# A transformer layer in fp32 on one core: the order of the first seven-fold products, the buffer of their first weight sum, and the place of eight transfers

## The chip, the core and the metric

The kernel runs on one core of one Trainium2 chip. Five engines work side by side, each through its own queue in order: PE (TensorE, matrix products), DVE (VectorE), ACT (ScalarE), POOL (GpSimd) and SP (SyncE, which here only issues transfers). POOL issues transfers too: all those that add what they carry to what lies at the target. The metric is the time of one execution in device microseconds (us); a lower one is better. Weights come from HBM (the chip's memory) in every execution.

## The reference

One layer on 512 tokens of width 2048, everything in float32, cut to what matters here:

```python
h = rms_norm(x, pre_mix_g)
z = h @ w_in                                  # [q | k | v | u], 4 x 1024 columns
a = chunked_attention(q, k, v, rel_bias)      # 8 heads
p = multiscale_pool(u, pool_w, pool_scale)    # 4 groups, windows 2, 4, 8, 16
x = x + rms_norm(concat(a, p) @ w_o, post_mix_g)
h = rms_norm(x, pre_ffn_g)
up = causal_dwconv(h @ w_up, conv_w, conv_b)  # w_up: 2048 x 11264
y = (gelu(up[..., :5632]) * up[..., 5632:]) @ w_down
x = x + rms_norm(y, post_ffn_g)
```

## The kernel before

**Numbers as pairs.** A float32 operand is split into a rounded high part and the rest: ACT writes the high part (L135, `activation` Copy), DVE subtracts it (L136). A product is then three matmuls (high by high, high by low, low by high), or two in the products of w_up. Every weight tile of 128x1024 numbers (512 KB) so costs one transfer into a raw buffer, one ACT instruction and one DVE instruction before PE can read it. Raw tiles of the tag `raw` (`raw4`, five buffers) and split halves of the tag `w4` (`w4`, eight buffers, so four pairs) are shared by all stages up to the products of w_up. A second set of raw buffers is `raw_x` (tag `x`, four buffers); the sums of h use it first, then the weights.

**Fewer products.** w_o, w_up and w_down are multiplied by the scheme of Strassen and Winograd: seven products of half-size blocks instead of eight, named by `i` = 1 to 7. Products 4, 5, 6 and 7 need sums of weight blocks. They are made in two ways:

- For w_o and for the first group of w_down, in HBM ahead of time by `sums_in_dram` (L296 on). It is a generator; each step is one transfer of 1 MB: a `copy`, issued by SP and tied behind the last weight load that SP issued (`issue_after(load_w.last)`), or an `add`, issued by POOL with `accum_op`. There are 32 steps for w_o (tile `wt`) and then 16 for w_down (tile `t`, `first_sum`): copies of sum 5 (2 steps, one for each half `cc` of the columns), adds to 5, copies of 7, copies of 6 from 5, adds to 7, adds to 6, copies of 4 from 6, adds to 4. The sums of w_down are read some 1000 us later. `more_sums(n)` takes n steps; the head loop takes the first 24.
- For w_up in SBUF by the class `Factors`. `k` numbers the 41 weight tiles that go through the scheme, `i` the product. For one `k`, the tile `x` is loaded by SP (L1089) and then added to by POOL (L1106), each time after the product's split has read the last state: product 1 reads the block as it is, 5 after one add, 6 after a second, 4 after a third. Products 3 and 7 share the tile `y` (one add between), product 2 reads `z`. Tiles `y` and `z` lie in `raw4`, `x` in `raw_x`. Only for the first and the last k (`alone`) is product 1 loaded by itself as `w`, since the order asks for 1 before the sum is there, and `x` starts with two blocks, the load and one add.

**Stages.** Projections of q, k and v with attention, head by head (to some 316 us); the eight projections of u with the pooling (`pool_proj`, `pool_keep`, `pool_mix`, to 409 us), whose running sums are chains of DVE additions with small POOL memsets between them (L488, L495); w_o (`wo_product`, seven products of two halves each, 409 to 562 us); the first three weight tiles of w_up without the scheme (`up`, to 644 us); then the loop over `factors.order`, "the sevens" (to some 1440 us); then w_down.

**The order around the change.** PE keeps the program's order; on the other engines a scheduler at build time orders instructions by when it expects them to be ready, the program's order deciding between them. In the sevens, `seven(k, i)` calls `factors.get`, which first emits the splits (`make`) up to four products ahead, then the matmuls; `keep(k, i)` after it empties the PSUM bank: after product 5 ACT copies bank `g` to `zb` (L1165), after product 6 bank `a` to `zm` (L1169). Product 3 adds onto bank `g` after product 5, product 7 onto bank `a` after 6, so each waits for that copy. The first six products are written out by hand in `begin`:

```python
begin = [(0, 1), (0, 2), (1, 1), (1, 2), (0, 5), (0, 3)]
```

and then come (0, 6), (0, 7), (1, 5), (0, 4), (1, 3), (2, 1), and so on. During the last plain product `up(1, 0)` the loads of the first six are issued and the splits of the first four made.

Of the kernel before, what the change touches and what calls it, by code (L numbers as in the profile page):

```python
# [75 lines left out]
def encoder_layer(ctx: ExitStack, tc: tile.TileContext, x, xT, vecs, rel, post_mix, post_ffn,  # L76
# [24 lines left out]
    def bank(name):  # L101
        return psum.tile([P, 512], F32, tag="ps", name=name)
# [4 lines left out]
    def raw4(name):  # L107
        return big.tile([P, 1024], F32, tag="raw", bufs=5, name=name)
# [41 lines left out]
    def mm3(ps, l, r, first, last, onto=False):  # L150
        nc.tensor.matmul(ps, l[0], r[0], start=first, stop=False, skip_group_check=onto)  # L151
        low = ps if len(r[1].shape) == 2 else ps.rearrange("p (a b) -> p a b", a=2)
        nc.tensor.matmul(low, l[0], r[1], start=False, stop=False, skip_group_check=onto)  # L153
        nc.tensor.matmul(ps, l[1], r[0], start=False, stop=last, skip_group_check=onto)  # L154
# [42 lines left out]
    def part(w, *idx):  # L197
        return tuple(v[(slice(None),) + idx] for v in w)
# [136 lines left out]
    for kb in range(KD):  # L335
        i, o = divmod(kb, 8)
        nc.sync.dma_start(xt[kb // 4][:, kb % 4, :], xT[kb * P:(kb + 1) * P, :])
        for what in "qk":
            if kb in chunks:
                raw, hi, lo = first[f"{what}0_{i}"]  # L340
# [18 lines left out]
    with tc.tile_pool(name="p1", bufs=2, reuse_waits="tile") as p1:  # L359
# [39 lines left out]
        def project(name, between=None):  # L399
            ps = bank(name)  # L400
            for i in range(2):
                if i and between:
                    between()
                w = weights.get(f"{name}_{i}")
                for j in range(8):
                    kb = 8 * i + j
                    mm3(ps, part(w, j), blk(hT, kb), kb == 0, kb == KD - 1)
            return ps
# [65 lines left out]
        def values(h):  # L474
            ps = bank(f"a{h}")
            d = slice((h % 4) * DH, (h % 4 + 1) * DH)
            for k in range(NT):
                sl = slice(PT_AT[k], PT_AT[k] + S - PT_Q[k])
                mm3(ps[:, PT_Q[k]:], part(state["v"], k, d), (pth[:, sl], ptl[:, sl]), k == 0, k == NT - 1)
            nc.scalar.activation(mix(h), ps, AF.Copy)  # L480

        def pool_proj(g, j):
            pool_keep(g, j, project(f"u{2 * g + j}"))
# [24 lines left out]
        def pool_mix(g, keep_):  # L508
            w = weights.get(f"pm{g}")
            d = [state.pop(("pool", g, a)) for a in range(2)]  # L510
            for j in range(2):
                ps = bank(f"pm{g}_{j}")
                for a in range(2):
                    mm3(ps, part(w, a, slice(j * P, (j + 1) * P)), d[a], a == 0, a == 1)
                keep_(HEADS + 2 * g + j, ps, col(V_PSCALE, 2 * g + j))
# [35 lines left out]
        def more_sums(n):  # L551
            for _ in range(n):
                next(sums_step, None)

        more_sums(2)
        pool_proj(0, 0)
        turn(6)
        scores(7)
        pool_proj(0, 1)
        more_sums(2)  # L560
        values(6)
        more_sums(2)
        pool_proj(1, 0)
        more_sums(2)
        turn(7)
        pool_proj(1, 1)
        more_sums(3)
        values(7)
        mixT += [acc8(f"mixT{i}", "B").rearrange("p (a b) -> p a b", a=4) for i in (2, 3)]
        pool_mix(0, keep_mix)  # L570
        more_sums(3)
        pool_proj(2, 0)
        more_sums(3)
        pool_proj(2, 1)
        pool_mix(1, keep_mix)
        more_sums(3)
        pool_proj(3, 0)
        more_sums(3)
        u7 = project("u7")


# [16 lines left out]
        def wo_product(i, cc, left, between=None):  # L598
            ps = [bank(f"m{i}{cc}{t}") for t in range(2)]
            if cc:  # L600
                more_sums(1)
            for q in range(4):
                w = weights.get(f"wo{i}_{cc}_{q}")
                for j in range(2):
                    kb = 2 * q + j
                    for t in range(2):
                        mm3(ps[t], tuple(v[:, kb, t * P:(t + 1) * P] for v in left), part(w, j), kb == 0, kb == 7)
                if between:
                    between(q)
            return ps  # L610
# [226 lines left out]
    def right(c, cc):  # L837
# [10 lines left out]
        while True:  # L848
            i = order
            if (c, (cc, i)) in ready_first:  # L850
                hi, lo = right_tile("wh", "bh"), right_tile("wl", "bl")
                for v, source in zip((hi, lo), ready_w[cc, i]):
                    with tc.issue_after(first_right.part) if first_right.part else nullcontext():
                        first_right.part = nc.gpsimd.dma_start(v, source.bitcast(F32R)).ins
                order = yield hi, lo
                continue
            if c == 0:

                v = first_right(cc, i, raw1 if (ORDER0.index((cc, i)) - len(ready_first)) % 5 < 3 else later["raw2"])
            else:  # L860
                for jl in {1: (11, 12), 6: (22,), 2: (21,)}.get(i, ()):
                    b[jl] = load(jl // 10 - 1, jl % 10 - 1)
                if i == 5:
                    nc.vector.tensor_add(b[11], b[11], b[12])
                if i == 7:
                    nc.vector.tensor_add(b[12], b[22], b[12])
                if i == 6:
                    nc.vector.tensor_add(b[11], b[11], b[22])
                if i == 4:
                    nc.vector.tensor_add(b[21], b[21], b[11])  # L870
                v = b[{1: 11, 5: 11, 7: 12, 6: 11, 2: 21, 3: 22, 4: 21}[i]]
            hi, lo = right_tile("wh", "bh"), right_tile("wl", "bl")
            split(hi, lo, v)
            order = yield hi, lo
# [71 lines left out]
    with tc.tile_pool(name="p3", bufs=2, reuse_waits="tile") as p3:  # L946
# [86 lines left out]
        def raw_x(name):  # L1033
            return p3.tile([P, 1024], F32, tag="x", bufs=4, name=name)
# [31 lines left out]
        class Factors:  # L1066
# [3 lines left out]
            def __init__(self):  # L1070
                n = 2 * NU - PLAIN

                self.alone = 0, n - 1
                place_of = {1: 0, 6: 8, 2: 2, 7: 10, 5: 4, 4: 12, 3: 6}
                begin = [(0, 1), (0, 2), (1, 1), (1, 2), (0, 5), (0, 3)]
                end = [(n - 1, 5), (n - 2, 6), (n - 1, 3), (n - 1, 1), (n - 2, 7), (n - 1, 6), (n - 2, 4),
                       (n - 1, 7), (n - 1, 2), (n - 1, 4)]
                order = sorted((7 * k + at, k, i) for k in range(n) for i, at in place_of.items())  # L1080
                self.order = begin + [(k, i) for _, k, i in order if (k, i) not in begin + end] + end
                self.raw, self.made, self.loaded, self.used = {}, [], 0, 0
# [4 lines left out]
            def load(self, k, i):  # L1087
                def raw(what, tile_, m, kh):
                    nc.sync.dma_start(tile_, self.block(k, m, kh))  # L1089
                    self.raw[k, what] = tile_  # L1090

                if i == 1 and (k, "w") not in self.raw:
                    raw("w" if k in self.alone else "x", raw4("wx") if k == self.alone[0] else raw_x("wx"), 0, 0)
                elif i == 5 and k == self.alone[0]:
                    raw("x", raw_x("wx"), 0, 0)
                    self.add(k, "x", 1, 0)
                elif i == 5 and k == self.alone[1]:
                    raw("w", raw_x("wx"), 0, 0)
                    raw("x", raw_x("wx"), 1, 0)
                elif i == 3:  # L1100
                    raw("y", raw4("wy"), 1, 1)
                elif i == 2:
                    raw("z", raw4("wz"), 0, 1)
# [137 lines left out]
    with tc.tile_pool(name="p4", bufs=2, reuse_waits="tile") as p4:  # L1241
# [19 lines left out]
        def left(c):  # L1261

            def load(i):
                g = half_g(f"gc{i}")
                nc.sync.dma_start(g, gd[c][i])
                return [g[:, :, j, :] for j in range(2)]

            i = yield
            a11, a12 = load(0)
            v = {1: a11, 2: a12}  # L1270
            while True:
                if 7 not in v and (c or i not in (1, 2)):
                    a21, a22 = load(1)
                    s = scratch("s")
                    v.update({5: s, 7: a21, 6: s, 3: s, 4: a22})
                if i == 5:
                    nc.vector.tensor_sub(s, a22, a21)
                if i == 6:
                    nc.vector.scalar_tensor_tensor(s, s, -1.0, a11, op0=ALU.mult, op1=ALU.subtract)
                if i == 3:  # L1280
                    nc.vector.scalar_tensor_tensor(s, a12, -1.0, s, op0=ALU.mult, op1=ALU.subtract)
                if i == 7:
                    nc.vector.tensor_sub(a21, a11, a21)
                hi, lo = slot_h("ah", F32R), slot_l("al", F32R)
                split(hi, lo, v[i])
                i = yield hi, lo
# [198 lines left out]
```

## Time and profile before

| | us |
|---|---|
| time, median of 3 runs | 1888.29 (1887.30 to 1889.62) |
| the profiled execution | 1887.21, span 1885.4 |
| PE busy / DVE busy / ACT busy / POOL busy | 1862.0 / 1438.4 / 1019.2 / 297.3 |
| PE idle from 380 to 560 us | 5.7 |
| PE idle from 645 to 690 us | 6.7 |
| PE idle from 690 to 1435 us | 0.0 |

How to read the rows below: a row of the timeline has its start and its duration in us, then engine, line, operation, output `<-` inputs and the number of instructions; in brackets the engine's idle time before it and what ended that. SPq is SP's queue, that is the issue of a transfer. The chain of waits has start, duration and what. A row of the waits has who waited for whom, the total in us, how many times, and the longest. A row of the windows has the stretch, its length, busy time and number of instructions of each engine, the granted clock of PE, the busy share of the 16 DMA engines and GB/s. A row of the transfers of a queue has packets, MB and the share of the 16 DMA engines in that stretch (q0: POOL's, q1: SP's); one of the issues has KB and the median us from issue to landing.

### The profile page before, as it was taken

How to read it: one execution, taken by the hardware profiler on the slowest of the kernel's cores; microseconds unless marked ns; L12 is line 12 of the kernel's file. 1: busy time of each engine (PE TensorE's matmuls, PEld its weight loads, DVE VectorE, ACT ScalarE, POOL GpSimd, SP SyncE). 2: the span in 40 equal slices, each digit the busy share in tenths (PEclk: the TensorE clock that was granted, in tenths of full speed). 3: DMA queues.
4: the chain of work that ended last, by engine and by line, in shares of the span. 5: the costliest groups of instructions: out<-in, count | busy, mean ns of one | idle time of the engine just before them, and what ended most of it. 6: DMA issues, size and time to landing. Idle time of an engine off the chain costs nothing.

```text
span 1885.4 us, 24890 instructions
## 1 busy us (share of the span) xinstructions
PE 1862.0 (99%) x9486; PEld 1591.7 (84%) x9486; DVE 1438.4 (76%) x1631; ACT 1019.2 (54%) x1287; POOL 297.3 (16%) x400
## 2 busy tenths in 40 slices
PE   9999999989999989999999999999999999999998
PEld 7888888868889878888888888888888888888886
DVE  5554446468598978888888888888887899889875
ACT  6433333246456456666656656665665765565553
POOL 4301011100000112222121221212211011111101
PEclk9999999999999999999999999999999999999999
DMA  8899599997665688989889888898988977877785
GB/s 293 250 252 238 155 274 273 255 246 248 222 222 202 166 185 197 200 199 209 208 196 204 200 205 202 200 211 199 204 187 275 351 233 179 204 201 174 176 236 151
DMA packets 181751, 409.20 MB, mean 217 GB/s; under 512 B 11456, under 2 KB 62528, under 8 KB 176320
## 3 DMA queue, kind: packets, MB, share of 16 engines
q0 software_dynamic: 52112, 156.78, 43.5%
q1 hardware_dynamic: 129520, 250.84, 39.8%
q8 instruction: 74, 1.21, 0.3%
q14 instruction: 45, 0.37, 0.1%
HBM read 361.44 MB, written 96.47 MB: 243 GB/s over the span
## 4 chain that ended last, share of the span: by engine, by line
PE 92%; DMA 3%; DVE 2%; issue 1%; ACT 1%; SPq 0%; POOL 0%; POOLq 0%; DVEq 0%; ACTq 0%
PE qa L159 16%; PE qa L165 8%; PE qg L159 8%; PE qg L165 4%; PE pa L151 4%; PE pa L154 4%; PE pa L153 4%; PE qd L159 4%; PE m L153 2%; PE m L154 2%; PE m L151 2%; PE qd L165 2%; PE pg L151 2%; PE pg L154 2%; PE pg L153 2%; PE v L153 2%
## 5 line engine op out<-in xcount | busy, mean ns | idle before, releaser
L135 ACT ACTIVATE wfh<-wx 128x1024 fp32r<-128x1024 f32 x164 | 173.7, 1059 | 137.6 <-PE qg L159 52.5
L159 PE MATMUL qa<-gT,wfh 128*128 128x512 f32 x984 | 246.4, 392 | 0.0
L136 DVE TENSOR_TENSOR wfl<-wx,wfh 128x1024 fp32r<-128x1024 f32 x164 | 200.5, 1222 | 57.7 <-ACT wfh L135 43.6
L159 PEld LDWEIGHTS qa<-gT,wfh 128*128 128x128 f32 x984 | 177.0, 189 | 31.7
L1106 POOL DMA_DIRECT2D wx<-in_w_up x122 | 104.6, 860 | 509.4 <-DVE wfl L136 447.0
L159 PE MATMUL qg<-h,wfh 128*128 128x512 f32 x656 | 163.6, 392 | 6.0 <-ACT zb L1165 6.0
L159 PEld LDWEIGHTS qg<-h,wfh 128*128 128x128 f32 x656 | 124.0, 189 | 32.0 <-ACT zb L1165 6.2
L136 DVE TENSOR_TENSOR bl<-b,bh 128x2048 fp32r<-128x2048 f32 x56 | 127.1, 2286 | 18.6 <-ACT bh L135 11.7
L165 PE MATMUL qa<-gT,wfl 128*128 128x256 f32 x984 | 137.8, 283 | 0.7 <-ACT zm L1169 0.7
L135 ACT ACTIVATE wfh<-wy 128x1024 fp32r<-128x1024 f32 x82 | 86.9, 1060 | 91.9 <-PE qg L159 54.6
L135 ACT ACTIVATE bh<-b 128x2048 fp32r<-128x2048 f32 x56 | 106.0, 1912 | 54.7 <-DVE b L870 22.5
L165 PEld LDWEIGHTS qa<-gT,wfl 128*128 128x128 f32 x984 | 129.4, 191 | 4.6 <-ACT zm L1169 1.3
L151 PE MATMUL pa<-bh,ah 128*128 128x512 f32 x320 | 124.5, 389 | 0.0
L153 PE MATMUL pa<-bl,ah 128*128 128x512 f32 x320 | 124.5, 389 | 0.0
L154 PE MATMUL pa<-bh,al 128*128 128x512 f32 x320 | 124.5, 389 | 0.0
L136 DVE TENSOR_TENSOR wfl<-wy,wfh 128x1024 fp32r<-128x1024 f32 x82 | 100.1, 1220 | 8.6 <-PE qa L159 2.9
L165 PEld LDWEIGHTS qg<-h,wfl 128*128 128x128 f32 x656 | 89.5, 190 | 6.5
L136 DVE TENSOR_TENSOR wfl<-wz,wfh 128x1024 fp32r<-128x1024 f32 x41 | 50.3, 1226 | 55.6 <-PE qa L159 55.6
L165 PE MATMUL qg<-h,wfl 128*128 128x256 f32 x656 | 91.5, 282 | 0.0
L159 PE MATMUL qa<-h,wfh 128*128 128x512 f32 x328 | 82.1, 392 | 0.0
L159 PE MATMUL qd<-gT,wfh 128*128 128x512 f32 x328 | 81.1, 389 | 0.0
L938 POOL DMA_DIRECT2D sum<-part x30 | 36.2, 1207 | 262.6 <-DVE part L924 190.3
(543 smaller groups left out, 4554.1 us busy)
## 6 DMA issues: line engine op xcount, KB each, us to landing
wx<-in_w_up POOLq DMA_DIRECT2D x122, 512.0 KB, 6.1
b<-in_w_down SPq DMA_DIRECT2D x32, 1024.0 KB, 7.0
wx<-in_w_up SPq DMA_DIRECT2D x43, 512.0 KB, 5.4
wz<-in_w_up SPq DMA_DIRECT2D x41, 512.0 KB, 5.9
wy<-in_w_up SPq DMA_DIRECT2D x41, 512.0 KB, 4.6
wy<-in_w_up POOLq DMA_DIRECT2D x41, 512.0 KB, 6.8
sum<-part POOLq DMA_DIRECT2D x38, 512.0 KB, 7.8
wt<-in_w_o POOLq DMA_DIRECT2D x16, 1024.0 KB, 12.7
```

Source lines behind the costliest of these rows:

```text
L135: rounded = nc.scalar.activation(hi, src, AF.Copy)
L136: rest = nc.vector.tensor_sub(lo, src, f32(hi))
L151: nc.tensor.matmul(ps, l[0], r[0], start=first, stop=False, skip_group_check=onto)
L153: nc.tensor.matmul(low, l[0], r[1], start=False, stop=False, skip_group_check=onto)
L154: nc.tensor.matmul(ps, l[1], r[0], start=False, stop=last, skip_group_check=onto)
L159: nc.tensor.matmul(ps, w[0][:, kb], pairs[kb][0], start=fresh and not kb, stop=last, skip_group_check=not fresh)
L165: nc.tensor.matmul(ps[:, sl], w[1][:, kb], pair[:, sl], start=False, stop=last, skip_group_check=not fresh)
L938: nc.gpsimd.dma_start(dest, v, accum_op=ALU.add)
L1106: nc.gpsimd.dma_start(self.raw[k, what], self.block(k, m, kh), accum_op=ALU.add)
```

## The change

Two things are edited. In the stages of u and w_o, `more_sums` is called with smaller numbers between the projections (16 steps there instead of 23), and the last eight steps are taken in the second halves of the w_o products, one in each, two in that of product 3 (before, one step was left for them). In the sevens, `begin` is reordered: (0, 5) comes third instead of fifth, and (1, 1) stands between (0, 5) and (0, 3); the tile `x` of k = 0 is taken from `raw4` instead of `raw_x`.

```diff
-        more_sums(2)
+        more_sums(1)
         pool_proj(0, 0)
...
         pool_proj(0, 1)
         more_sums(2)
         values(6)
-        more_sums(2)
+        more_sums(1)
         pool_proj(1, 0)
         more_sums(2)
         turn(7)
         pool_proj(1, 1)
-        more_sums(3)
+        more_sums(2)
         values(7)
...
         pool_mix(0, keep_mix)
-        more_sums(3)
+        more_sums(2)
         pool_proj(2, 0)
-        more_sums(3)
+        more_sums(2)
         pool_proj(2, 1)
         pool_mix(1, keep_mix)
-        more_sums(3)
+        more_sums(2)
         pool_proj(3, 0)
-        more_sums(3)
+        more_sums(2)
         u7 = project("u7")
...
             if cc:
-                more_sums(1)
+                more_sums(2 if i == 3 else 1)
...
-                begin = [(0, 1), (0, 2), (1, 1), (1, 2), (0, 5), (0, 3)]
+                begin = [(0, 1), (0, 2), (0, 5), (1, 1), (0, 3), (1, 2)]
...
                 elif i == 5 and k == self.alone[0]:
-                    raw("x", raw_x("wx"), 0, 0)
+                    raw("x", raw4("wx"), 0, 0)
                     self.add(k, "x", 1, 0)
```

## The prediction

> **What bounds the kernel now.** First the page's busy times, then who PE waited for over the whole run, then windows around those waits.
>
> ```profile
> PE 1862.0 (99%) x9486; PEld 1591.7 (84%) x9486; DVE 1438.4 (76%) x1631; ACT 1019.2 (54%) x1287; POOL 297.3 (16%) x400
> ...
> PE qg L159 <- ACT zb L1165: 6.0, 1, 6.0
> PE u L151 <- ACT u_1h L135: 1.5, 1, 1.5
> PE m L153 <- DVE wo_2l L136: 1.4, 1, 1.4
> PE u L154 <- DVE u_1l L136: 1.3, 2, 0.8
> PE m L151 <- ACT wo_2h L135: 1.1, 1, 1.1
> PE qa L165 <- ACT zm L1169: 0.7, 1, 0.7
> PE m L153 <- DVE wo_1l L136: 0.5, 1, 0.5
> ...
> 386.00:422.00 36.00, 30.26 (x122) 0.95 0.95 264
> 657.00:672.00 15.00, 8.27 (x41) 0.77 0.84 179
> ...
> 690.00:1435.00 745.00, 745.00 (x4282) 657.90 (x4281) 619.54 (x728) 453.38 (x553) 162.49 (x196) 1.00 0.88 200
> ```
>
> PE is busy 1862.0 of 1885.4 us, and from 690 to 1435 us without a gap. So only time at which PE stands still, or runs with a lower granted clock, can be won. Apart from the start and the tail, that lies in two places, and each edit touches one: 386 to 422 us (u's last projections, w_o's first product; clock 0.95) and 657 to 672 us (the start of the sevens; clock 0.77).
>
> **What the first place costs.** Five of the waits lie there: 1.5 + 1.3 + 0.5 + 1.1 + 1.4 = 5.7 us (1.3 are two waits, so six gaps). A matmul of 512 columns is written 0.39 long but the next starts 0.23 after it, so each gap of the profile hides another 0.16, and the first matmul after it takes about 0.1 more: 6 x 0.26 = 1.6 us. After the last one the clock is down:
>
> ```profile
> 420.00 0.43 PE m L153
> ...
> 422.29 0.23 PE m L154
> ```
>
> From 418.9 to 421.1 the steps are 0.43 instead of 0.23, some seven of them with the partial ones: 1.5 us. Together 8.8 us.
>
> **What it comes from.** SP's queue and POOL's queue, in order, around 343 to 402:
>
> ```profile
> SPq L300 <- DMA t<-in_w_down: 15.7, 3, 8.9
> ...
> 358.93 27.79 DMA u_1r<-in_w_in
> ...
> 387.93 0.50 PE L151 MATMUL u<-hT,u_1h 128*128 128x512 f32 x1 [1.46 <-ACT u_1h L135]
> ...
> q1 hardware_dynamic: 425, 0.21, 12.2%
> ...
> 397.99 1.16 POOL L303 DMA_DIRECT2D t<-in_w_down  x1 [19.23 <-DMA t<-t]
> ...
> 400.20 1.16 POOL L303 DMA_DIRECT2D t<-in_w_down  x1 [0.94 <-DMA t<-t]
> 401.94 0.11 POOL L488 MEMSET u<- 128x16 f32 x1 [0.48 <-DVE tmp L500]
> 399.29 0.70 DVE L493 TENSOR_TENSOR us<-us 128x524 f32<-128x524 f32 x1 [5.93 <-POOL us L495]
> ```
>
> The copies of sum 6 from 5 stand in SP's queue until the adds to 5 have landed (15.7 us in all), and the load `u_1r` of the seventh u projection, queued behind them, goes out at 358.93 and lands 27.79 later, at 386.7; PE needs it at 386.5 (387.93 less the wait). It is slow since two adds are in flight: from 376 to 384 us (the row q1) SP's queue gets 12.2% of the DMA engines and moves 0.21 MB, at which pace 512 KB take 20 us. Then the memset of a pooling chain stands behind an add that waits 19.23 us for its copy, and DVE, in order, idles 5.93 us for it. From 399.3 DVE is late; w_o's splits, and behind them PE, wait for that.
>
> **Part 1, the transfers.** After the edit the copies stand elsewhere in SP's queue: those of 5 behind the u load behind which those of 7 stand now, those of 7 behind the last u load, those of 6 behind the first load of w_o, those of 4 in w_o's products 6 and 3. Adds are tied to nothing but their copies: the one at 400.20 belongs, by the program, to w_o's product 1 and still stands ahead of a memset of the pooling before it. So I expect the adds to go as copies land, and only the two copies and two adds of sum 4 truly move into w_o. What matters is that nothing stands ahead of `u_1r` any more. Its buffer is free from
>
> ```profile
> 347.39 1.22 DVE L136 TENSOR_TENSOR u_1l<-u_1r,u_1h 128x1024 fp32r<-128x1024 f32 x1 [1.34 <-ACT u_1h L135]
> ```
>
> on, so it goes out at 348.6. If it again takes 27.8 it is there at 376.4, ten before PE asks. DVE then does not idle the 7.9 us for its split (380.0 to 387.9) nor most of the 5.93, and is some ten ahead where it was late. I take 7.9 of the 8.8 and leave 0.9 for a split that still comes late among DVE's work in w_o's first product. Bounds: 8.8, if nothing is left; 4.4, if the waits for wo_1 and wo_2 stay (3.0, their hidden part 0.8, and a part of the clock's); 0, if the crowd on the DMA engines is as before: counted by the program's steps, nine of ten copies and of ten adds stay between u's second projection and w_o's first product.
>
> The cover of the moved ones: w_o's loads.
>
> ```profile
> 503.00:545.00 42.00, 42.00 (x187) 34.75 (x187) 31.33 (x27) 20.59 (x26) 0.00 (x0) 1.00 0.56 181
> ...
> 506.31 0.38 SPq L146 DMA_DIRECT2D wo_0r<-in_w_o  x1
> 517.53 1.06 ACT L135 ACTIVATE wo_0h<-wo_0r 128x1024 fp32r<-128x1024 f32 x1 [1.66 <-PE m L153]
> 525.72 0.39 PE L151 MATMUL m<-wo_0h,s 128*128 128x512 f32 x1
> ...
> q0 software_dynamic: 594, 1.18, 83.5%
> q1 hardware_dynamic: 295, 0.58, 23.9%
> ...
> wo_1r<-in_w_o SPq DMA_DIRECT2D x1, 512.0 KB, 12.3
> ```
>
> A load goes out 19.4 us before its matmul, its two splits take 2.3, so it may take 17.1 to land. The last three rows are from 402 to 410, w_o loads under two adds: at most 12.3 us. An add of 1 MB takes 1 / 1.18 x 8 = 6.8 us, in which SP moves one load instead of the 2.5 that PE uses (one in 2.7 us): 4.1 us late, a copy the like, and the DMA engines are 44% idle to catch up. Price 0; without that cover, 4 us for each. POOL's only other work there, the two norms, is wanted after the last add, and the copies that move wait for adds issued some 100 us before, so SP's queue does not stand.
>
> **Part 2, the sevens.**
>
> ```profile
> 649.39 2.00 PE L159 MATMUL qa<-gT,wfh 128*128 128x512 f32 x8
> 652.18 2.00 PE L159 MATMUL qd<-gT,wfh 128*128 128x512 f32 x8
> ...
> 663.97 3.55 PE L159 MATMUL qg<-h,wfh 128*128 128x512 f32 x8 [6.04 <-ACT zb L1165]
> ...
> 638.81 1.04 ACT L135 ACTIVATE wfh<-wx 128x1024 fp32r<-128x1024 f32 x1
> ...
> 657.45 1.06 ACT L135 ACTIVATE wfh<-wx 128x1024 fp32r<-128x1024 f32 x1 [4.47 <-DMA wx<-in_w_up]
> 660.02 1.06 ACT L135 ACTIVATE wfh<-wy 128x1024 fp32r<-128x1024 f32 x1 [1.52 <-DMA wy<-in_w_up]
> ...
> 663.34 0.57 ACT L1165 ACTIVATE zb<-qg 128x512 f32<-128x512 f32 x1
> ...
> 608.13 6.00 SPq L1089 DMA_DIRECT2D wz<-in_w_up  x2
> 636.78 9.19 SPq L1089 DMA_DIRECT2D wx<-in_w_up  x3
> 641.86 1.86 POOL L1106 DMA_DIRECT2D wx<-in_w_up  x2 [36.30 <-DMA wx<-in_w_up]
> DMA to landing us min/median/max: 5.5/7.8/9.4
> ```
>
> A product takes 2.79 us (652.18 - 649.39). The copy `zb` of (0, 5) stands on ACT behind the splits of (0, 6) and (0, 7), which wait for adds (657.45, 660.02), and PE, at 657.8 done with (0, 5), waits until 663.97: 6.04, 0.16 hidden, and 8 matmuls at the lower clock, 3.55 instead of about 2.0: 7.8 us.
>
> After: the tile of (0, 5) takes the raw buffer that frees third, at 613.8 (second of the `wz` issues at 608.13), not 636.8, and POOL, idle 36.30 us there, adds its second block by some 625. Its split comes in third place (638.81, DVE's half done by 642.2); its next add is issued at 642.3 and lands 5.5 to 9.4 later (last row, that tile from 640 to 660 us): 647.8 to 651.7. (0, 5) runs 649.4 to 652.2, PE having begun the sevens at 643.8 (two products earlier), and the last split ahead of `zb` on ACT is that of (0, 6): done by 652.8, `zb` by 653.4. PE has (1, 1) in between and asks for it at 655.0: no wait, 1.6 us to spare. The same products in the same number: nothing is added.
>
> What is late next: (0, 7) behind `zm` (0.7 us now). Ahead of that copy stand the splits of (0, 4), after an add issued at about 655 ((0, 6)'s split, 2.3 on ACT and DVE, done by 654, then POOL), so there at 660.5 to 664.4, and of (1, 3); 2.1 us for both, so `zm` could start at 662.6 to 666.5 and PE is done with (0, 6) at 663.4. From 0 to 3.1 us; at the median landing of 7.8, 1.5. I take 0.7, between the least and the median: 7.1 won. Bounds 8.6 (the 0.7 of `zm` goes too) and 4.7. The buffer of `raw` that the sum holds until (0, 4) is split is missed only by loads for the eighteenth product and later, which PE reaches past 690 (643.8 + 17 x 2.79): nothing.
>
> [...]
>
> **The sum.** 7.9 + 7.1 = 15.0 us. The profiled execution took 1887.2 (span 1885.4 and 1.8 around it): 1872.2. The median of the three runs, 1888.3, is 1.1 above it: **1873.3 us**. With the bounds 4.4 + 4.7 and 8.8 + 8.6 the likeliest case lies from 1871 to 1879.
>
> **The rivals.** (a) Part 1 gives nothing: the crowd holds `u_1r` up all the same. For it: nine of ten copies and adds stay; against it: the copies that held SP's queue are no longer ahead. 1888.3 - 7.1 = 1881.2. (b) Part 2 only moves the wait to another copy behind a late add (`zm`, or `zb` if an add takes over 11 us): for it the 1.5 us at the median; against it the 1.6 to spare at the slowest add. If all 7.8 come back: 1880.4. (c) Slower: the moved transfers hold w_o's loads as they held `u_1r`. A landing of 27.8 us is 10.7 over the 17.1 that a load has, and PE waits that long at each such meeting; from two on (21.4, over 15.0 + 3.8) the kernel is slower than before: 1894.7. Against it: the 12.3 us of the w_o load, under two adds. [...] (d) The scheduler orders the queues anew and both gains go: 1888.
>
> **How the numbers follow.** Forecast 0.58, (a) 0.14, (b) 0.10, (d) 0.08, (c) 0.10. The range 1869.5 to 1884 holds the forecast, (a) and (b), 0.82. A measurement can tell about 0.2% (3.8 us) from no change: faster (under 1884.5) 0.82, same 0.08, slower 0.10.
>
> **What would show it.** Right: no PE wait for `u_1h`, `u_1l` or `zb`; `u_1r` issued near 349, with no `t<-t` ahead of it; (0, 6)'s split before `zb`, not after a 4 us wait; sums of 4 moved behind 500 us with PE unbroken; 690 to 1435 as before, only 15 earlier. Wrong: a DMA as the releaser of a `wo` split; POOL's memsets still behind an add for over 5 us; a new wait at `zm` of over 2 us.

## The result, and the profile after

| | before | after |
|---|---|---|
| median, 6 runs each | 1888.52 us (1887.30 to 1889.62) | 1876.55 us (1874.32 to 1878.70) |
| ratio, 95% interval | | 0.9937 [0.9925, 0.9950] |
| the profiled execution (span) | 1887.21 (1885.4) | 1878.70 (1876.9) |

12.0 us were won; the forecast was 1873.3 us, 15.2 under the median of before. The profiled execution after is the slowest of its six, 2.2 us over their median, and its losses are to be read with that in mind. First who PE waited for after, then the windows of after: the two places, and the long stretch behind them, moved forward by the lead that PE has there.

```profile
PE qa L165 <- ACT zm L1169: 4.7, 2, 3.7
...
PE up L153 <- DVE gT L139: 0.8, 1, 0.8
```

```profile
386.00:422.00 36.00, 36.00 (x160) 29.83 (x159) 33.68 (x44) 18.35 (x22) 2.91 (x10) 1.00 0.91 229
657.00:672.00 15.00, 12.65 (x56) 10.92 (x57) 10.92 (x15) 7.90 (x10) 2.57 (x3) 0.77 0.71 137
680.00:1426.00 746.00, 744.98 (x4278) 657.39 (x4277) 619.65 (x728) 452.11 (x553) 162.00 (x195) 1.00 0.88 199
```

The waits for `u_1h`, `u_1l`, `wo_1`, `wo_2` and `zb` are gone, and 386 to 422 us has neither a gap nor a low clock. The second place still has both (clock 0.77): `zm` stands where `zb` stood. Comparing the start of PE's n-th matmul in the two traces gives the lead of after: 8.7 us from 425 us on, 7.9 from 590 us (the wait for `gT`, at the norm behind w_o), 10.1 at 680 us, 9.7 by 1390 us, and 8.5 at the end (another 1.0 of waiting for `zm` at 1404 us, behind an add that took 8.4 us to land). So the transfers gave 8.7, the sevens 2.2, and 2.4 were lost again elsewhere.

The timeline of the moved transfers after, with what stood behind them (SP's, POOL's, DVE's rows):

```profile
348.77 0.37 SPq L146 DMA_DIRECT2D u_1r<-in_w_in  x1
...
370.68 1.64 SPq L300 DMA_DIRECT2D t<-t  x2
...
385.83 1.16 POOL L303 DMA_DIRECT2D t<-in_w_down  x1 [13.12 <-DMA t<-t]
...
388.10 1.16 POOL L303 DMA_DIRECT2D t<-in_w_down  x1 [1.00 <-DMA t<-t]
...
387.13 0.70 DVE L493 TENSOR_TENSOR us<-us 128x524 f32<-128x524 f32 x1 [5.47 <-POOL us L495]
...
504.07 1.16 POOL L303 DMA_DIRECT2D t<-in_w_down  x1 [94.89 <-DMA t<-t]
525.62 1.16 POOL L303 DMA_DIRECT2D t<-in_w_down  x1 [20.39 <-DMA t<-t]
```

`u_1r` goes out at 348.8. The adds to 6 (385.83, 388.10) go as their copies land, only the sums of 4 lie in w_o. But POOL still stands 13.12 us at an add, and DVE still idles 5.47 us for the memset behind it, hardly less than the 5.93 of before. What differs is when that ends: 387.1 instead of 399.3 us.

The start of the sevens after: ACT's rows, then PE's, then the pieces of the chain of waits that lead to them.

```profile
655.41 1.52 ACT L950 ACTIVATE ca<-z,vec 128x512 f32<-128x512 f32 x2 [3.12 <-DMA gd<-ca]
656.83 1.04 ACT L135 ACTIVATE wfh<-wx 128x1024 fp32r<-128x1024 f32 x1
657.78 1.04 ACT L135 ACTIVATE wfh<-wy 128x1024 fp32r<-128x1024 f32 x1
658.73 0.57 ACT L1169 ACTIVATE zm<-qa 128x512 f32<-128x512 f32 x1
...
653.66 2.00 PE L159 MATMUL qa<-h,wfh 128*128 128x512 f32 x8
659.35 2.07 PE L165 MATMUL qa<-gT,wfl 128*128 128x256 f32 x8 [3.69 <-ACT zm L1169]
661.22 3.62 PE L159 MATMUL qa<-gT,wfh 128*128 128x512 f32 x8
```

```profile
647.82 7.48 DMA gd<-ca
...
656.92 1.89 ACT wfh L135 x2
```

PE has finished (0, 6) at 655.5. The copy `zm`, in ACT's queue, stands behind two taps of the second gate (L950) and the splits of (0, 4) and (1, 3). (A gate is made of what a product of w_up gives by a short convolution, begun on ACT by the two instructions called taps here, and then a Gelu.) The taps write the only buffer of the tag `ca`, and wait until the first gate is stored from it (the `gd` piece, 7.48 us). PE waits 3.69 us, and the 16 matmuls behind that run at a granted clock of 0.50 (659 to 664 us; 2.07 instead of 1.11 for eight of 256 columns, 3.62 instead of 2.00 for eight of 512): 3.69 + 0.16 hidden + 2.6 = 6.5 us.

### The profile page after: what moved, and what is told of

It reads as the page before. It is cut to its first block, busy times and chain, and to the rows that moved or that the text cites. A ratio compares the mean times of both kernels' runs of the same rounds, so it can differ in the third digit from the quotient of the medians.

```text
span 1876.9 us, 24890 instructions
## 1 busy us (share of the span) xinstructions
PE 1860.8 (99%) x9486; PEld 1592.3 (85%) x9486; DVE 1439.5 (77%) x1631; ACT 1018.8 (54%) x1287; POOL 297.9 (16%) x400
## 4 chain that ended last, share of the span: by engine, by line
PE 64%; issue 2%; DMA 1%; ACT 0%; DVE 0%; POOL 0%; POOLq 0%; DVEq 0%; ACTq 0%
PE qa L159 16%; PE qa L165 8%; PE qg L159 8%; PE qg L165 4%; PE pa L154 4%; PE pa L153 4%; PE pa L151 4%; PE qd L159 4%; PE pg L154 2%; PE pg L153 2%; PE pg L151 2%; PE qd L165 2%; PE pd L154 1%; PE pd L153 1%; PE pd L151 1%
## 5 line engine op out<-in xcount | busy, mean ns | idle before, releaser
L136 DVE TENSOR_TENSOR bl<-b,bh 128x2048 fp32r<-128x2048 f32 x56 | 127.2, 2287 | 18.7 <-ACT bh L135 11.7
```

The lines of the kernel that those rows point to most:

```text
L136: rest = nc.vector.tensor_sub(lo, src, f32(hi))
```

## The experiments

Each ran beside the kernel before on the same chip (medians of before there: 1886.9, 1887.2 and 1886.9 for e1 to e4, e5 to e8 and e9 to e12). A ratio of 0.001 is 1.9 us.

| | median us | ratio to before, 95% interval |
|---|---|---|
| e1 transfers only | 1879.76 | 0.9961 [0.9948, 0.9973] |
| e2 sevens only (order and buffer) | 1883.85 | 0.9986 [0.9977, 0.9995] |
| e3 order only | 1891.14 | 1.0017 [1.0008, 1.0026] |
| e4 buffer only | 1885.52 | 0.9991 [0.9982, 1.0000] |
| e5 (0, 6) ahead of (1, 2) | 1875.47 | 0.9939 [0.9927, 0.9952] |
| e6 second gate in its own buffer | 1875.10 | 0.9939 [0.9926, 0.9951] |
| e7 copies of 6 back | 1878.40 | 0.9955 [0.9943, 0.9968] |
| e8 last eight steps at once | 1890.88 | 1.0019 [1.0010, 1.0028] |
| e9 `zm` ahead of two splits | 1874.90 | 0.9937 [0.9925, 0.9950] |
| e10 `zm` ahead of two taps | 1872.44 | 0.9924 [0.9911, 0.9936] |
| e11 `zm` ahead of both | 1875.84 | 0.9942 [0.9928, 0.9956] |
| e12 before, memsets on DVE | 1880.48 | 0.9968 [0.9956, 0.9981] |

### Do the parts add up (e1, e2)

e1 is before with the `more_sums` numbers of the change, e2 before with `begin` and `raw4("wx")` of the change.

> The edit to the transfers alone; the sevens as before. Theory (the two parts add up, each in its own place): the waits for u_1h, u_1l and wo_* are gone, which gave 8.7 us of lead by 425 us in the changed kernel's trace, of which 0.9 went at the norm behind w_o, so 1888.5 - 8.7 + 0.9 = 1880.7 us, and PE still waits some 6 us for zb. Rival A (the sevens eat part of a lead that comes from earlier stages, since their loads wait for transfers and not for PE): a longer zb wait than 6.0 and 1883 us or more.

> The edit to the sevens alone (order and buffer); the transfers as before. Theory (the wait moves from zb to zm, because two tap instructions of the second gate and two splits stand ahead of that copy on ACT): no wait for zb, a wait for zm of 3 to 4 us, the slow clock behind it, and 1888.5 less 2.2 to 4.2, so 1884.3 to 1886.3 us; the lost u_1r waits stay. Rival B (the record's sizing: zm costs 0.7): 1881.4 us and a wait for zm under 1.5 us.

The waits of PE in e1 and in e2:

```profile
PE qg L159 <- ACT zb L1165: 5.9, 1, 5.9
```

```profile
PE qa L165 <- ACT zm L1169: 2.9, 1, 2.9
PE u L151 <- ACT u_1h L135: 2.0, 1, 2.0
PE m L153 <- DVE wo_2l L136: 1.4, 1, 1.4
```

By the ratios e1 wins 7.4 us and keeps the whole `zb` wait, e2 wins 2.6 and keeps the waits around u. Together 10.0, beside 11.9 for both at once; the intervals, some 2.4 and 1.7 us to each side, hold the difference. The parts are separate, and rival A falls. The sevens alone win far less than the 7.1 of the prediction (in e2's trace, the fastest of its eleven, PE gains 4.0 us there, from 643 to 690 us) and lose the rest to `zm`, whose 2.9 us are just under the 3 to 4 expected: rival B falls too.

### Order or buffer (e3, e4)

```diff
-                    raw("x", raw4("wx"), 0, 0)
+                    raw("x", raw_x("wx"), 0, 0)
...
-                begin = [(0, 1), (0, 2), (0, 5), (1, 1), (0, 3), (1, 2)]
+                begin = [(0, 1), (0, 2), (1, 1), (1, 2), (0, 5), (0, 3)]
```

These are the lines as against e2: the first makes e3, the second e4.

> The new order of the first products, transfers as before, and the first sum in the old buffer (raw_x). Theory (the sum must be there early, and only the other buffer brings it): the load of (0, 5) goes out near 637 us as before, its split is done near 650 us, the add for (0, 6) lands near 657 us, and PE waits 3 to 6 us for zb or zm: 1886.5 to 1890 us. Rival C (the order does it alone): as the order and the buffer together, 1884.3 to 1886.3 us.

> The old order, transfers as before, and the first sum in the other buffer. Theory (the order is needed too): the split of (0, 5) no longer waits 1.7 us for its add, so that the add for (0, 6) lands 1.7 us earlier and the zb wait is 4.3 instead of 6.0 us: 1886.8 us. Rival D (without the order the earlier sum is worth nothing): 1888.5 us; rival E (the buffer does it alone, no zb wait): under 1884 us.

The waits of PE at the sevens in e3, then in e4:

```profile
PE qa L165 <- ACT zm L1169: 8.5, 2, 8.0
PE qg L159 <- ACT zb L1165: 1.7, 1, 1.7
```

```profile
PE qg L159 <- ACT zb L1165: 6.5, 1, 6.5
```

Each alone leaves the wait where it is or makes it longer: with the order alone the sum is late, every add behind it too, and e3 is slower than before, also than was expected of it. e4's ratio is the one expected (0.9991), but not for the reason given: its wait of 6.5 contradicts the expected 4.3. That e4 is 1.7 us faster than before rests on an interval that touches 1, and its trace is 2.2 us ahead already at 425 us, where the edit does nothing.

### What holds zm (e5, e6, e9, e10, e11)

All five are the changed kernel with one more edit. e5 puts a product between (0, 6) and the one that needs `zm`, e6 frees the taps from the store:

```diff
-                begin = [(0, 1), (0, 2), (0, 5), (1, 1), (0, 3), (1, 2)]
+                begin = [(0, 1), (0, 2), (0, 5), (1, 1), (0, 3), (0, 6), (1, 2)]
...
-            if u == NU - 1:
+            if u == 1:
+                a = raw_x("ca").rearrange("p (a b) -> p a b", a=2)
+            elif u == NU - 1:
```

> The changed kernel with (0, 6) ahead of (1, 2), so that a product that needs no copy lies between (0, 6) and (0, 7). Theory (PE waits for zm only because (0, 7) follows (0, 6) at once, while two taps and two splits stand ahead of that copy): no wait for zm over 1 us at the start of the sevens, no slow clock there, and the 6.5 us that these cost in the changed kernel's trace are won, at its median perhaps 4.3: 0.9903 to 0.9915 of the time before. Rival F (the adds are what is late: the wait goes on to the next split behind an add): a wait for a wfh of over 2 us, and 0.993 to 0.995.

> The changed kernel with the second gate's tile in a buffer of its own (raw_x), so that its two taps on ACT need not wait for the store of the first gate. Theory (of the 3.3 us that zm stands behind PE some 2.6 come from those taps): they run near 650 us, zm starts near 656 instead of 658.7, PE waits some 1.2 us instead of 3.7 and the clock stays up: 0.991 to 0.993 of the time before. Rival G (the two splits behind the add of (0, 4) set zm, not the taps): the wait stays over 2.5 us and the time is the changed kernel's, 0.993 to 0.995.

ACT and PE in e5; then in e6:

```profile
657.60 0.57 ACT L1169 ACTIVATE zm<-qa 128x512 f32<-128x512 f32 x1
...
658.23 1.85 PE L165 MATMUL qa<-gT,wfl 128*128 128x256 f32 x8 [2.52 <-ACT zm L1169]
659.88 2.95 PE L159 MATMUL qa<-gT,wfh 128*128 128x512 f32 x8
```

```profile
655.06 1.06 ACT L135 ACTIVATE wfh<-wx 128x1024 fp32r<-128x1024 f32 x1 [1.29 <-DMA wx<-in_w_up]
656.03 1.03 ACT L966 ACTIVATE ca<-ca 128x1024 f32<-128x1024 f32 x1
656.97 1.04 ACT L135 ACTIVATE wfh<-wy 128x1024 fp32r<-128x1024 f32 x1
657.92 0.58 ACT L1171 ACTIVATE zm<-qa 128x512 f32<-128x512 f32 x1
...
658.55 1.22 PE L165 MATMUL qa<-gT,wfl 128*128 128x256 f32 x8 [2.54 <-ACT zm L1171]
659.60 2.00 PE L159 MATMUL qa<-gT,wfh 128*128 128x512 f32 x8
```

Both expectations fail: neither kernel is faster than the change (0.9939 each, beside 0.9937). In e5 PE leaves (0, 6) 2.8 us earlier, but `zm` is copied when ACT comes to it, at 657.6, behind the taps, the store that they wait for and one split: PE's order does not set it. (The sign of rival F, a wait of PE for a `wfh`, does not appear.) In e6 the taps run early; then the split of (0, 4), behind its add, the second gate's Gelu (L966) and the split of (1, 3) stand ahead of `zm`. Taking one thing away from the head of ACT's queue let the scheduler put another there. Both signs of rival G are met, a wait over 2.5 us and the time of the change; but with the Gelu moved in as well, e6 cannot tell whether the taps or the splits hold `zm` in the changed kernel. So the copy's place itself was fixed, by tying behind it the splits (e9), the taps (e10), or both (e11):

```diff
-                nc.scalar.activation(v, banks[k, "a"], AF.Copy)
+                keep.zm = nc.scalar.activation(v, banks[k, "a"], AF.Copy).ins
...
+                    if len(self.made) in (9, 10):
+                        behind.enter_context(tc.issue_after(keep.zm))
+                    split(hi, lo, v)
...
-                self.prefetch(n)
+                self.prefetch({6: 3, 7: 2}.get(self.used, n))
...
-        gates[1] = gate(1, normed(z))
+        z = normed(z)
...
+            if (k, i) == (0, 6):
+                with tc.issue_after(keep.zm):
+                    gates[1] = gate(1, z)
```

The first three pieces make e9 (by the third, the `prefetch` line, the two splits are emitted after (0, 6)); the first and the last two make e10; all make e11.

> The changed kernel with the splits of (0, 4) and (1, 3) tied behind the copy zm of (0, 6); the two taps of the second gate still stand ahead of it. Theory (each of the two holds zm): the taps, which wait for the store of the first gate until some 655.4 us, end at 656.8, PE waits 1.8 us for zm instead of 3.7, and with a slow clock behind it or without, 1.8 to 4.5 us are won against the changed kernel's trace: 0.992 to 0.9935 of the time before. Rival L (the splits do not count): wait and time as in the changed kernel.

> The changed kernel with the second gate's taps tied behind zm; the two splits still stand ahead of it. Theory: the split of (0, 4) starts when its add has landed (654.0 us in the changed kernel's trace), both splits end near 656, PE waits about 1 us for zm and the clock stays up: 0.991 to 0.993. Rival M (the taps do not count): wait and time as in the changed kernel, 3.7 us and 0.993 to 0.995.

> The changed kernel with both the taps and the two splits tied behind zm. Theory (ACT's order is all there is to it): zm starts as PE ends (0, 6), PE waits 0.7 us, no slow clock, and some 5.6 us are won against the changed kernel's trace, 3.6 against its median: 0.991 to 0.9925 of the time before, the record's 1873.3 us within 2 us. Rival N (what is pushed back is late next): a wait of over 1 us for a wfh or wfl, for zb, or for ca within the next 30 us, and no gain.

PE at its wait for `zm` in e9, in e10, and twice in e11, there with the ACT row that ends the second one:

```profile
656.80 1.21 PE L165 MATMUL qa<-gT,wfl 128*128 128x256 f32 x8 [1.31 <-ACT zm L1172]
```

```profile
655.48 1.22 PE L165 MATMUL qa<-gT,wfl 128*128 128x256 f32 x8 [0.69 <-ACT zm L1169]
```

```profile
656.00 1.22 PE L165 MATMUL qa<-gT,wfl 128*128 128x256 f32 x8 [0.69 <-ACT zm L1172]
...
675.52 1.06 ACT L135 ACTIVATE wfh<-wx 128x1024 fp32r<-128x1024 f32 x1 [3.54 <-DMA wx<-in_w_up]
...
677.82 1.22 PE L165 MATMUL qa<-gT,wfl 128*128 128x256 f32 x8 [2.08 <-ACT zm L1172]
```

The taps count most: with them behind, the wait is 0.69 us, as in the kernel before, and the two splits ahead cost nothing, since the add of (0, 4) lands in time (its split starts at 652.32, 2.5 us before `zm`). In e10's trace a lead of 8.7 us at 643 us becomes 16.5 at 690 us and stays. With the splits behind, 1.31 stay, and e9 is no faster than the change: its lead of 14.1 us at 690 us is down to 12.0 at 1430 us. e11 has the short wait too, but rival N is there as well, with `zm` as the tile waited for: the splits pushed back push the adds that POOL issues after them (the next two go out at 662.20 and 664.26 instead of 656.41 and 660.78 in e10), and the next `zm`, at 677 us, stands behind a split that waits for such an add. e10 is the fastest of all, 14.3 us under before. Its interval overlaps with the change's own, so that it beats the change is likely, not shown.

### What made PE wait at 386 to 422 us (e7, e8, e12)

e7 counts the steps so that the copies of 5, 7 and 6 stand where before has them, and those of 4 do not; e8 has everything of the change up to the copies of 6, and the last eight steps at once behind u; e12 is the kernel before with the memsets of the pooling chains on another engine:

```diff
 e7, from pool_proj(0, 0) on
-        more_sums: 1, 2, 1, 2, 2, 2, 2, 2, 2
+        more_sums: 2, 2, 2, 2, 3, 3, 3, 1, 0
 e8
         u7 = project("u7")
+        more_sums(8)
 e12
-            nc.gpsimd.memset(u[:, :PAD], 0.0)
+            nc.vector.memset(u[:, :PAD], 0.0)
...
-                    nc.gpsimd.memset(nxt[:, :step], 0.0)
+                    nc.vector.memset(nxt[:, :step], 0.0)
```

> The changed kernel with its steps counted so that the copies of 5, 7 and 6 stand in SP's queue where they stood before; those of 4 stay in w_o. Theory (the place of the copies of 6 does it: SP stands until the adds to 5 have landed, and u_1r behind them is late): u_1r goes out near 359 us, PE waits for u_1h or u_1l and then for wo_2, and 6 to 8 us of the gain go: 0.9965 to 0.9985 of the time before. Rival H (the number of transfers there does it, and with the copies of 4 and their adds gone the rest is harmless): no such waits, 0.993 to 0.995.

> The changed kernel with its last eight steps taken at once behind u's last projection, so that the copies of 4 stand in SP's queue ahead of most of w_o's first loads, and everything up to the copies of 6 stays. Theory (a copy that waits for an add holds whatever is queued behind it): the copies of 4 wait for the adds to 6, until some 395 us, w_o's fourth load goes out only then, and PE waits 3 to 10 us for wo splits: 0.9955 to 0.9995 of the time before. Rival I (w_o's loads have cover enough, only the place of the copies of 6 counts): no wait for wo, 0.993 to 0.995.

> The kernel before, with the small memsets of the pooling chains on DVE instead of POOL, so that none stands behind an add; transfers and sevens as before. Theory (two losses lie at 386 to 422 us: the late u_1r, and POOL's adds ahead of the memsets; the second makes the waits for wo_*): the waits for wo_1 and wo_2 and the slow clock behind them go, those for u_1h and u_1l stay, 4 to 6 us are won: 0.9968 to 0.998 of the time before. Rival O (the late u_1r alone makes DVE late): the wo waits stay, 0.999 or more.

e7: SP's waits at 330 to 450 us, its issue of `u_1r`, DVE's longest idle time, and the window:

```profile
SPq L300 <- DMA t<-in_w_down: 14.1, 2, 8.2
```

```profile
357.95 0.54 SPq L146 DMA_DIRECT2D u_1r<-in_w_in  x1
...
387.85 1.23 DVE L136 TENSOR_TENSOR u_0l<-u_0r,u_0h 128x1024 fp32r<-128x1024 f32 x1 [6.83 <-ACT u_0h L135]
```

```profile
386.00:422.00 36.00, 36.00 (x160) 29.81 (x160) 32.66 (x43) 19.96 (x24) 0.65 (x7) 1.00 0.55 176
```

SP stands nearly as long as before (14.1 beside 15.7), `u_1r` goes out at 358 again and takes 18.0 us, the load behind it makes DVE idle 6.83 us, and PE does not wait at all. With the copies of 4 and the adds to 4 out of the stage, DVE catches up in time, and at 425 us e7 is 9.1 us ahead of before. The theory, that the place of the copies of 6 by itself does it, falls, though the load was not as slow here as the 27.8 us of before. The ratio, 0.9955, lies between what the theory and rival H expected, some 3 us behind the change (0.9937). The two intervals overlap, and e7's one trace shows nothing that would cost it; whether the late loads cost something in other executions is open.

e12: the one wait of PE there, DVE's idle time, and POOL at the add to 4:

```profile
PE m L153 <- DVE wo_2l L136: 0.5, 1, 0.5
```

```profile
391.18 1.23 DVE L136 TENSOR_TENSOR u_0l<-u_0r,u_0h 128x1024 fp32r<-128x1024 f32 x1 [9.88 <-ACT u_0h L135]
...
396.56 1.16 POOL L303 DMA_DIRECT2D t<-in_w_down  x1 [19.34 <-DMA t<-t]
```

No transfer is moved here; POOL stands 19.34 us at the add as before (19.23). But nothing of the pooling is behind it, and 6.0 us are won, where moving the transfers (e1) wins 7.4. Rival O falls. The other half of the theory did not come either: the waits for `u_1h` and `u_1l` are gone too. In this execution `u_1r` took 19.5 us, so e12 says nothing on a load as late as that of before. e4, which has the transfers of before, shows the same from the other side, on DVE, POOL and PE:

```profile
380.58 1.23 DVE L136 TENSOR_TENSOR u_1l<-u_1r,u_1h 128x1024 fp32r<-128x1024 f32 x1 [0.26 <-ACT u_1h L135]
...
398.46 0.70 DVE L493 TENSOR_TENSOR us<-us 128x524 f32<-128x524 f32 x1 [13.56 <-POOL us L495]
...
397.16 1.16 POOL L303 DMA_DIRECT2D t<-in_w_down  x1 [18.06 <-DMA t<-t]
...
400.36 0.80 PE L154 MATMUL u<-hT,u_1l 128*128 128x512 f32 x1 [2.96 <-DVE u_1l L136]
```

In that execution `u_1r` took 18.7 us, about as in e7, its split ran at 380.6 in good time, and DVE then idled 13.56 us for a memset behind the add to 4, the next `u_1l` stood behind that, and PE waited for it. e8 is the extreme: the copies of 4 wait in SP's queue for the adds to 6, so the adds to 4 come later still, and again a memset is behind (POOL, DVE, PE):

```profile
408.48 1.16 POOL L303 DMA_DIRECT2D t<-in_w_down  x1 [19.21 <-DMA t<-t]
...
415.93 0.70 DVE L493 TENSOR_TENSOR us<-us 128x524 f32<-128x524 f32 x1 [19.84 <-POOL us L495]
...
417.82 0.79 PE L154 MATMUL m<-wo_0h,a 128*128 128x512 f32 x1 [10.91 <-DVE a L136]
```

The 10.91 us are waited for `a`, the left factor of w_o, whose split stands behind the pooling on DVE, not for a w_o load; 1.3 more for `wo_2l` and a clock of 0.83 from 386 to 422 us make up the rest of the 16 us by which e8 is behind the change at 425 us. It is more than was expected, and by another queue.

## Why the prediction was right or wrong

**The sum.** 15.0 us were forecast and 12.0 came, inside the range. Part 1 was 7.9; 8.7 are in the trace of after, and 7.4 in e1. Part 2 was 7.1; 2.2 are in that trace, 4.0 in e2's (2.6 by e2's ratio), and 11.9 - 7.4 = 4.5 by the ratios of the change and e1. The miss lies in part 2.

**Part 1, the size, was right; its leading cause was not.** The step that failed: "What matters is that nothing stands ahead of `u_1r` any more." In e7 the load stands behind the copies of 6 as before, and PE waits for nothing; in e4 its split is in time, and PE waits all the same; e12 leaves the queue as it was and wins 6.0 us. The late load did cost something of its own: PE's waits of 1.46 and 0.52 us at 388 and 389 us in before, and of 1.99 and 0.52 there in e2, the two traces in which it took some 28 us; in e3, e4, e7 and e12, where it took 18 to 22, these two waits are missing. The larger cause is the one that the prediction named second, for the 5.93 us of DVE alone: adds in POOL's queue, waiting for their copies, with a memset behind them that DVE needs. The change helps since the last adds ahead of that memset are now those to 6 and not those to 4, so that DVE goes on at 387.1 and not 399.3. That the size came out is in part luck: one edit removes both causes. The prediction's own sign against it, memsets behind an add for over 5 us, did appear (5.47), without a cost to PE: a stall in itself says little, what counts is when it ends. What the place of the copies of 6 is worth beside this, some 3 us by e7, is not clear of noise.

**That the adds go as copies land, and the price of 0 in w_o,** were right. From 480 to 545 us the slowest loads of w_o after took

```profile
DMA to landing us min/median/max: 4.7/6.0/10.8
```

us (tile `wo_3r`), under the 17.1 that they have, and PE waited for none. At the start of w_o, where the prediction did not look, `wo_1r` took 17.0 us beside two copies and the adds, and was in time all the same. The prediction's rival (c), w_o loads held by transfers, did not come. e8 is slower, but through the memset.

**Part 2: `zb` was right, `zm` was the term mis-sized.** No wait for `zb`; the split of (0, 5) at its early place, the add of (0, 4) landed at 654.0 (issued 646.45, 7.5 to landing), as early as the prediction's 660.5 to 664.4 with 7.8 us of lead taken off. From there the prediction counted only the two splits, 2.1 us, and took 0.7 us for the lateness of `zm`, on top of the 0.7 that PE waits for it anyway. It left out the two taps of the second gate, which stood in ACT's queue of before too, ahead of `zb`, and did not ask what they wait for (the store `gd`). They end at 656.8, the splits 1.9 later, and PE waits 3.69 us, 3.0 more than before, with 2.6 of slow clock behind it: 5.6 us where the sum had 0.7. Of the 7.8, 2.2 are left, which is what the trace shows. That is the prediction's rival (b) in most of its size, and its sign for it, a wait at `zm` of over 2 us; but what holds the copy is the taps behind a store, not a late add. With the taps behind the copy (e10) part 2 comes true: 0.69 us of wait, 7.7 won in the sevens and 14.3 in all, of the 15.0. e10 is one step more than the change.

**The rest.** The wait for `gT` behind w_o was not foreseen: 0.8 us here, 0.5 to 0.7 in e1, e5 and e9, none in e6, e7, e10 and e11. From 690 to 1435 us it is as before but for the 1.0 at 1404 and 0.4 of lead that goes earlier. The prediction's rival (d) did not come: both gains are in e1 and e2 apart.

**The clock.** Among what can be won the prediction counted 1.5 us of slow matmuls at 419 us, behind waits of 1.1 and 1.4 us. In before the granted clock is 0.50 from 418 to 421 us; after, with the waits gone, it is 1.00 from 386 to 422 us and no slow matmul is left there. That waits like these bring the slow clock each time is not so: e3 has them too (0.5, 1.0 and 1.4 us) and no slow matmul behind them.

## What to carry to other kernels

Where an engine both issues transfers that wait for others and does small work for a chain, look at what is queued behind the waiting issue, and price it by the time at which the last one ends, not by how long it stands. When a product is moved earlier, list everything that stands ahead of the next copy in its engine's queue, other phases' instructions included, each with what it waits for. Freeing one of them can let another take its place, as in e6; fixing the place of the copy itself, and no more than that, was the surer edit here.

## What the runs showed of the hardware

Waits of one length were followed by a slow clock in one run and not in another. The same matmul behind the same wait, in before and in e3:

```profile
418.35 0.80 PE L153 MATMUL m<-wo_2l,a 128*128 128x512 f32 x1 [1.41 <-DVE wo_2l L136]
```

```profile
416.75 0.50 PE L153 MATMUL m<-wo_2l,a 128*128 128x512 f32 x1 [1.41 <-DVE wo_2l L136]
```

In before the next six are written 0.63 to 0.52 us long, in e3 0.40 and 0.39. At the sevens it is 2.52 us of waiting in e5 (then 1.85 and 2.95 us for 1.2 and 2.0), 2.54 in e6 (1.22 and 2.00, none), 2.85 in e2 (3.56, slow), 2.08 in e11 (none). So the length of the wait alone does not decide it; what else does, these runs do not show.

The same load at the same place of SP's queue, `u_1r` issued at 357.5 to 358.9 us, took 27.8, 28.4, 22.0, 18.7, 18.0 and 19.5 us to land in before, e2, e3, e4, e7 and e12. POOL issues its next two adds at 371 to 376 us in all six. What makes the difference no run tests.
